# Projections of a hybrid decoder step: the two halves of the tokens in step, or one after the other

## The chip, the core and the metric

The program runs on one core of one Trainium2 chip. The metric is the device time of one execution in microseconds (us). TensorE (PE) multiplies, VectorE (DVE), ScalarE (ACT) and GpSimd (POOL) work elementwise, and SyncE (SP) starts the transfers. Every engine takes its instructions in one fixed order.

## What is computed

Two layers of a decoder trunk over 512 prompt tokens and 8 single-token samples, 1024 features wide, all in fp32. Cut to what matters here:

```python
for l in range(DEPTH):                                   # 2
    mod = silu(c) @ ada_w[l] + ada_b[l]                  # conditioning: shift, scale, gate
    h = rms_norm(x, norm_g[l]) * (1 + scale) + shift
    pa, pb, pc, pd = split(h @ w_in[l])                  # ONE input projection, 1024 -> 3648 columns
    oA = mixer_hgrn2(pa)                                 # A: chunked gated recurrence
    oB = mixer_rwkv7(pb)                                 # B: state update per token
    oC = mixer_dilated(pc)                               # C: windowed attention
    oD = mixer_pool(pd)                                  # D: pooling
    x = x + gate * (concat(oA, oB, oC, oD) @ w_out[l])   # ONE output projection, 1024 -> 1024
```

## The kernel before

Features lie on partitions and tokens along the free axis: the 512 prompt tokens and the 8 samples make 520 columns, cut into two halves of 256 and 264 (`HALF`). The input projection is cut into 29 column tiles of 128 features (`TILES`; the first, `wa`, has 64), the output projection into 8. A column tile sums over 8 feature tiles k of the input. Each fp32 operand is the sum of two parts, so one (half, k) step is three matmuls: `whi` against `hh`, `whi` against `hl`, `wlo` against `hh` (in the output projection `mh`, `ml` take the place of `hh`, `hl`). A whole column tile is 2 halves x 8 k x 3 = 48 matmuls into two PSUM tiles, one per half (`pj`; three such buffers, `pj_ps`).

Weights arrive by DMA in pieces of four k (`wraw`, six buffers). ACT copies a piece to `whi`, POOL subtracts to get `wlo` (`w_split`, L436 to L451); of either there are three buffers. So a column tile uses two pieces, k 0 to 3 and k 4 to 7, and a buffer is free again when the last matmul that reads its piece is through.

`project` (L458) issues one column tile and yields now and then the time that its matmuls take by plan, in ns. `Flow` (L124) is the planner: it lays the tensor engine's work in one order, the projections between the steps of the mixers. A mixer step of cost c allows 1.11 c ns of projection (`RATIO`, `debt`), and the projections' yields are taken from that allowance and added to the planner's clock, by which a mixer step counts as ready. Behind the planner a scheduler orders each engine's queue once more by its own estimate of when operands and buffers are there. So a change in `project` moves instructions on all engines.

When the 29 tiles are through, the projections wait for the event "mixed" (mixers A and B finished), then run the output projection over the first four k (the features of A and B), tile by tile; the last four k (C and D) come after all mixers have ended. The first layer's first seven column tiles are made in two passes of four k each (`split_projections`). Where two tiles go together (a layer's first group) `project` takes another branch.

Names of PE's instructions below: `bA` are the products of mixer B's chunks, `bR`, `bU`, `bS`, `by` the steps of its loop over 8 chunks, `bs` and `bss` sums over a head's features, `cs`, `cT`, `co` the scores, transposes and values of attention (C), `alv`, `adg`, `ao`, `sBa` parts of A and of the samples' step.

Of the kernel before, what the change touches and what calls it, by code (L numbers as in the profile page):

```python
# [18 lines left out]
PSUM = bass.MemoryType.PSUM  # L19
# [23 lines left out]
# column offsets of the parameters that sit one value per partition  # L43
# [9 lines left out]
# column tiles of the input projection, in the order in which they are made  # L53
# [70 lines left out]
class Flow:  # L124
    """Lays the tensor engine's work out in one order: projections, which are always ready, between the
    steps of the mixers, each of which waits for other engines."""
# [9 lines left out]
    def add(self, gen, prio=0):  # L136
        # priority, time when its data is there, awaited event, steps, whether it can rest here
        self.streams.append([prio, 0.0, None, gen, True])
        self.streams.sort(key=lambda e: e[0])
# [32 lines left out]
    def run(self):  # L172
        """Until the projections are through and every stream has ended."""
        while self.pj is not None or self.streams:
# [4 lines left out]
            ready = [e for e in self.streams if self._ready(e)]  # L179
# [12 lines left out]
def trunk(ctx: ExitStack, tc: tile.TileContext, I, O):  # L192
# [70 lines left out]
    def logistic(t):  # L263
        """1 / (1 + t), in place, for t = exp(-x)."""
        act(t, t, AF.Ln, bias=1.0)
        act(t, t, AF.Exp, scale=-1.0)
# [16 lines left out]
    C = {}  # L283
# [45 lines left out]
    def small_params():  # L329
        # lower bounds: cumulative softmax over the layers, minus the first layer's share  # L330
# [21 lines left out]
    modA, modS, modG = {}, {}, {}  # L352

    def ada_part(l, f0, nf, spare=0, ahead=1, pin=False):
        """Part of the conditioning, features on partitions: the shifts and scales of the feature tiles
        f0 .. f0 + nf - 1, or all the gates (nf = 8); groups of columns side by side. pin keeps the
        order of the trace, for loads that come later than the scheduler takes them to."""
# [7 lines left out]
        # a single tile: the even and the odd k side by side as well  # L365
# [35 lines left out]
        # a group is a kind of two features (nf = 4), or else one or two features of a kind  # L401
# [18 lines left out]
    def w_extend(groups, halves=(0, 1)):  # L420
        """Weight tiles [128, (k, m)] in the order of use; each comes in two halves of k."""
# [14 lines left out]
    def w_split(upto):  # L436
        """Each weight as the sum of two parts that one pass each carries."""
# [20 lines left out]
    def project(group, xt, each_k=None, k0=0, k1=8):  # L458
        """One or two column tiles, both halves of the tokens; each operand as two exact parts."""
# [3 lines left out]
        def step(i, hf, k):  # L463
# [5 lines left out]
            # a narrow tile has both parts of its weights side by side in hi  # L469
# [15 lines left out]
        else:  # L485
            step(0, 0, k0)
            yield 330.0
            for k in range(k0, k1):
                if k < k1 - 1:
                    step(0, 0, k + 1)  # L490
                step(0, 1, k)
                yield 660.0
# [10 lines left out]
    def split(hi, lo, src, eng=V):  # L503
        """Write src as the sum of two parts that one pass each carries."""
        copy(hi, src)
        sub(lo, src, hi.bitcast(F32), eng=eng)

    def evac(dst, halves):
        """Copy both halves out of PSUM, one on each of two engines."""
# [5 lines left out]
    def blk_sum(src, use, on=False):  # L515
        """Sum over the 64 features of each head, spread over them; use(psum, index). The operand goes in as
        two exact parts."""
# [21 lines left out]
    def to_tm(dst, src, other):  # L539
        """Tokens on partitions: dst[p][(., t), (c, th), d], in squares of 32; the rows are those of the head's  # L540
        parity p, or the other half."""
# [10 lines left out]
    def to_tokens(dst, src):  # L552
        """Tokens on partitions: dst[t, tile of 128 tokens, (th, p, d)]."""
# [12 lines left out]
    def scols(ap, i):  # L566
        """[.., th, b] spread over the values of batches 4 i .. 4 i + 3."""
# [3 lines left out]
    def sample_values(v, dr):  # L571
        """The samples' values [(p, v), th, b] on every partition of their parity, [(p, .), b, th, v] for four
        samples at a time, by way of DRAM."""
# [15 lines left out]
    def sample_queries(q):  # L589
        """Each sample's query per head, with zeros in the other head's rows."""  # L590
# [6 lines left out]
    def sample_read(S, z):  # L597
        """o[(p, v), th, b] = sum over keys of S[(p, key), b, th, v] q[(p, key), th, b]; both th against the
        queries of both, of which each takes its own."""
# [11 lines left out]
    # =====================================================================  # L611
# [27 lines left out]
    def again(src):  # L639
        """What waited in DRAM comes back."""  # L640
# [22 lines left out]
    def stream_A(l, L, flow):  # L663
# [4 lines left out]
        # each chunk's queries, per head with zeros in the other head's rows  # L668
# [26 lines left out]
        # the samples' step reads q, f and k as they come  # L695
# [68 lines left out]
        for cp in range(2):  # L764
            # within the chunks, and from the states before them
# [35 lines left out]
    def shift_mix(l, L, xs, dd, rows, col):  # L801
        """x + (previous token - x) * mu, into dd."""
# [28 lines left out]
    def stream_B(l, L, flow):  # L831
        yield "wa"
        a, sg = fm("ba"), fm("bsg")
        # both low ranks with their exact parts one above the other: rows hi, lo, hi against weights hi, hi, lo
# [20 lines left out]
        # decays within a chunk, relative to the chunk's middle  # L855
# [26 lines left out]
        # normalised removal key  # L882
# [14 lines left out]
        # a Newton step: the errors of the removal add up over the tokens  # L897
# [13 lines left out]
        # bonus  # L911
# [6 lines left out]
        # the samples' step  # L918
# [808 lines left out]
def pack(inp):  # L1727
# [9 lines left out]
    d = {}  # L1737
# [96 lines left out]
```

## Time and profile before

| | |
|---|---|
| Device time, median of 3 runs | 782.69 us (782.3 to 784.27) |
| Profiled execution: span from first to last instruction | 781.0 us |
| Its own device time | not listed apart from the three runs |
| Mean granted TensorE clock | 0.956 |
| PE busy | 715.5 us (92%) |
| DVE, POOL, ACT busy | 593.2 (76%), 384.7 (49%), 365.2 us (47%) |

The profile gives the busy time of each engine, its waits by what ended them, and a line of the granted clock. Times of rows are microseconds from the span's start. A matmul's row lasts 0.28 us while the next one starts 0.12 us later, since matmuls are pipelined. What PE delivers is read from the distance of starts, not from a row's duration.

### The profile page before, as it was taken

The page shows a single profiled execution, that of the slowest core. Times are in us where ns is not written, and L with a number is a line of the kernel's source. Part 1 is how long each engine was busy: PE and PEld are TensorE (multiplying, and loading weights), DVE is VectorE, ACT ScalarE, POOL GpSimd, SP SyncE. Part 2 cuts the span into 40 slices and gives each one's busy share as a digit, 9 for nine tenths or more (in the row PEclk, how much of TensorE's full clock was granted, in tenths as well). Part 3 has the DMA queues.
Part 4 walks back from the last instruction along what each step waited for, and adds up shares of the span by engine and source line. Part 5 has one row for each costly group of instructions (what it writes and reads, how often), then busy time and mean ns, then how long its engine had stood idle before and what let it go on. Part 6 is the DMA issues. An engine that isn't in the chain of part 4 may idle for free. (4 is left out here: it accounts for less than half of the span.)

```text
span 781.0 us, 18348 instructions
## 1 busy us (share of the span) xinstructions
PE 715.5 (92%) x7297; PEld 626.3 (80%) x7297; DVE 593.2 (76%) x1263; ACT 365.2 (47%) x778; POOL 384.7 (49%) x348
## 2 busy tenths in 40 slices
PE   2999989698789999999998999879889999999998
PEld 1687769487779998787888989768778989777898
DVE  4558759999998465788747897986999765587873
ACT  5233667014243465674235688412233547477520
POOL 2335427874753243236637756686554332223662
PEclk9999999897899999999998999899889999999999
DMA  9979755152232155337263323515232134135222
GB/s 330 351 276 335 226 168 153 41 163 69 82 98 56 40 183 192 125 97 272 69 190 96 118 68 98 147 56 150 69 95 86 56 99 150 56 113 163 98 77 102
DMA packets 67446, 105.74 MB, mean 135 GB/s; under 512 B 18336, under 2 KB 26848, under 8 KB 67360
## 3 DMA queue, kind: packets, MB, share of 16 engines
q1 hardware_dynamic: 67216, 104.50, 41.8%
q8 instruction: 57, 0.93, 0.5%
q14 instruction: 29, 0.24, 0.1%
q10 hardware_dynamic: 144, 0.06, 0.0%
HBM read 88.20 MB, written 14.22 MB: 131 GB/s over the span
## 5 line engine op out<-in xcount | busy, mean ns | idle before, releaser
L237 POOL TENSOR_TENSOR wlo<-wraw,whi 128x512 fp32r<-128x512 f32 x144 | 203.1, 1416 | 235.4 <-ACT whi L261 203.8
L269 PE MATMUL pj<-hh,whi 128*128 128x256 f32 (+1 forms) x928 | 278.0, 308 | 17.9 <-DVE raw L632 6.9
L269 PE MATMUL pj<-hl,whi 128*128 128x256 f32 (+1 forms) x928 | 268.3, 296 | 0.6 <-DVE hl L254 0.6
L269 PE MATMUL pj<-hh,wlo 128*128 128x264 f32 (+1 forms) x896 | 262.2, 298 | 0.5 <-POOL wlo L237 0.5
L269 PEld LDWEIGHTS pj<-hh,whi 128*128 128x128 f32 x928 | 182.3, 200 | 36.1 <-issue 12.6
L269 PEld LDWEIGHTS pj<-hl,whi 128*128 128x128 f32 x928 | 183.1, 200 | 4.6 <-issue 2.7
L269 PEld LDWEIGHTS pj<-hh,wlo 128*128 128x128 f32 x896 | 176.3, 199 | 6.2 <-issue 4.1
L261 ACT ACTIVATE whi<-wraw 128x512 fp32r<-128x512 f32 (+1 forms) x146 | 90.6, 623 | 161.5 <-PE pj L269 128.6
L269 PE MATMUL pj<-ml,whi 128*128 128x264 f32 (+1 forms) x256 | 72.5, 286 | 2.0 <-DVE cst L250 1.4
L269 PE MATMUL pj<-mh,whi 128*128 128x256 f32 (+1 forms) x256 | 72.6, 291 | 0.3 <-ACT mh L261 0.3
L269 PE MATMUL pj<-mh,wlo 128*128 128x256 f32 (+1 forms) x256 | 71.5, 283 | 0.0
L237 POOL TENSOR_TENSOR gate<-gate,raw 128x520 f32<-128x520 f32 x16 | 22.1, 1383 | 69.9 <-ACT gate L258 34.3
L254 DVE SCALAR_TENSOR_TENSOR x<-pj,mod,x 128x256 f32<-128x256 f32 x64 | 30.8, 481 | 33.1 <-PE pj L269 32.7
L269 PEld LDWEIGHTS pj<-mh,whi 128*128 128x128 f32 x256 | 47.4, 188 | 4.8 <-issue 2.6
L269 PEld LDWEIGHTS pj<-ml,whi 128*128 128x128 f32 x256 | 48.2, 188 | 3.3 <-DVE ml L237 2.7
L269 PEld LDWEIGHTS pj<-mh,wlo 128*128 128x128 f32 x256 | 48.0, 188 | 0.6 <-POOL wlo L237 0.4
L269 PE MATMUL ada<-adaw,sc 128*32 128x256 f32 (+1 forms) x448 | 33.9, 375 | 11.9 <-DVE nacc L237 11.8
L269 PEld LDWEIGHTS ada<-adaw,sc 128*32 128x32 f32 x448 | 12.4, 115 | 20.6 <-DVE nacc L237 11.8
L269 PE MATMUL alv<-aqz,ak 128*64 128x64 f32 x384 | 20.6, 249 | 6.6 <-DVE ak L237 6.6
L254 DVE SCALAR_TENSOR_TENSOR bX<-bX,bfac,bS 64x64 f32<-64x64 f32 x56 | 15.6, 279 | 14.2 <-PE bS L269 12.8
L269 PEld LDWEIGHTS alv<-aqz,ak 128*64 128x64 f32 x384 | 17.2, 157 | 10.0 <-issue 4.5
L1123 DVE COPY bUV<-bU 64x128 f32<-64x128 f32 x16 | 4.7, 295 | 23.3 <-ACT bUV L261 23.1
(409 smaller groups left out, 1456.1 us busy)
## 6 DMA issues: line engine op xcount, KB each, us to landing
wraw<-in_w_in_dram SPq DMA_DIRECT2D x112, 256.0 KB, 2.8
adaw<-in_ada_w_dram SPq DMA_DIRECT2D x48, 512.0 KB, 5.5
wraw<-in_w_out_dram SPq DMA_DIRECT2D x32, 256.0 KB, 2.8
x<-in_x_dram SPq DMA_DIRECT2D x8, 520.0 KB, 5.8
ckT<-in_ckT_dram SPq DMA_DIRECT2D x8, 320.0 KB, 3.2
x<-xmid SPq DMA_DIRECT2D x4, 520.0 KB, 5.8
cvr<-in_cvr_dram SPq DMA_DIRECT2D x4, 512.0 KB, 5.3
xmid<-x SPq DMA_DIRECT2D x7, 260.0 KB, 2.0
```

The lines of the kernel that those rows point to most:

```text
L237: return eng.tensor_tensor(out=out, in0=a, in1=b, op=op)
L254: return V.scalar_tensor_tensor(out=out, in0=a, scalar=s, in1=b, op0=op0, op1=op1)
L261: return A.activation(out, a, AF.Copy)
L269: return PE.matmul(out, lhsT, rhs, start=start, stop=stop)
L1123: V.tensor_copy(UV[ROWS[1], 1], pv[ROWS[1]])
```

## The change

In `project`, for a single column tile: before, the first half's step runs one k ahead of the second half's, so that both halves go through k together, offset by one. Now all k of the first half run, and then all k of the second half. The plan's yields change with it: before 330 and then eight times 660 (5,610 ns for a tile of 8 k; 2,970 for 4 k), now 660 after every second k (5,280 and 2,640). The rest of the diff takes out comments and does not change the program.

```diff
         else:
-            step(0, 0, k0)
-            yield 330.0
-            for k in range(k0, k1):
-                if k < k1 - 1:
-                    step(0, 0, k + 1)
-                step(0, 1, k)
-                yield 660.0
+            for hf in range(2):
+                for k in range(k0, k1):
+                    step(0, hf, k)
+                    if k % 2:
+                        yield 660.0
```

The same matmuls are issued, as many of each kind. Where they stand is seen in the order of the instructions. First PE in layer 0, between two groups of B's products (`bA`), in the kernel before; `pj_1926` and `pj_1927` are the two halves of one column tile:

```order
L269 MATMUL bA<-bZ_1694,bk 64x128
L269 MATMUL pj_1926<-hh_200,whi 128x256
L269 MATMUL pj_1926<-hl_202,whi 128x256
L269 MATMUL pj_1926<-hh_200,wlo 128x256
L269 MATMUL pj_1927<-hh_200,whi 128x264
L269 MATMUL pj_1927<-hl_202,whi 128x264
L269 MATMUL pj_1927<-hh_200,wlo 128x264
```

The same place in the kernel after; `pj_1914` is a second half:

```order
L269 MATMUL bA<-bZ_1731,bk 64x128
L269 MATMUL pj_1914<-hh_200,whi 128x264
L269 MATMUL pj_1914<-hl_202,whi 128x264
L269 MATMUL pj_1914<-hh_200,wlo 128x264
L269 MATMUL pj_1914<-hh_200,whi 128x264
L269 MATMUL pj_1914<-hl_202,whi 128x264
L269 MATMUL pj_1914<-hh_200,wlo 128x264
L269 MATMUL bA<-bZ_1728,bk 64x128
```

The alternation of the halves is gone, and mixer steps now stand inside one half. The second place is PE near the end of layer 1's attention, in the kernel before; `pj_9189`, `pj_9190` and `pj_9250` belong to the output projection:

```order
L269 MATMUL cs<-ckl,cqs 128x512
L1244 MATMUL cT<-c_ident,cS 128x128 x4
L269 MATMUL pj_9189<-ml_9184,whi 128x256
L269 MATMUL pj_9189<-mh_9183,wlo 128x256
L269 MATMUL pj_9190<-ml_9184,whi 128x264
L269 MATMUL pj_9190<-mh_9183,wlo 128x264
...
L269 MATMUL pj_9250<-mh_9183,wlo 128x256
L269 MATMUL co<-cPT,cvtm 64x128 x2
```

And in the kernel after, the end of a run that began 22 rows earlier with `cT` behind `pj_9197`:

```order
L269 MATMUL cs<-ckl,cqs 128x512
L1242 MATMUL cT<-c_ident,cS 128x128 x4
L269 MATMUL co<-cPT,cvtm 64x128 x2
L1242 MATMUL cT<-c_ident,cS 128x128 x6
L269 MATMUL co<-cPT,cvtm 64x128 x4
L1242 MATMUL cT<-c_ident,cS 128x128 x8
L269 MATMUL co<-cPT,cvtm 64x128 x6
L269 MATMUL pj_9160<-mh_9154,whi 128x256
```

There attention's steps stand with projections between them before, and without any now: 81 matmuls of the mixers in a row (34 `cT`, 30 `co`, 12 `cs`, 5 sums), and in layer 0 at the same place 75 (28 `cT`).

## Rows read from the trace of the kernel before

**Rows 1.** The page: busy time, and the granted clock in 40 slices (tenths).

```profile
PE 715.5 (92%) x7297; PEld 626.3 (80%) x7297; DVE 593.2 (76%) x1263; ACT 365.2 (47%) x778; POOL 384.7 (49%) x348
...
PEclk9999999897899999999998999899889999999999
```

**Rows 2.** Stages: stretch, length, busy PE, PEld, DVE, ACT, POOL, then clock.

```profile
113.00:243.00 130.00, 112.30 (x1345) 99.71 (x1344) 124.10 (x200) 44.38 (x85) 82.14 (x71) 0.89 0.34 100
243.00:317.00 74.00, 73.35 (x926) 63.63 (x924) 42.08 (x124) 38.24 (x93) 23.90 (x18) 1.00 0.38 120
317.00:368.00 51.00, 50.27 (x366) 41.10 (x365) 44.44 (x122) 35.55 (x89) 21.41 (x15) 0.97 0.51 171
...
480.00:608.00 128.00, 113.18 (x1308) 103.31 (x1306) 115.05 (x191) 46.31 (x87) 80.09 (x71) 0.91 0.33 98
...
684.00:736.00 52.00, 50.55 (x375) 41.49 (x371) 43.20 (x121) 36.33 (x90) 20.04 (x15) 0.97 0.42 138
```

**Rows 3.** PE's waits over the whole span: us in total, times, longest.

```profile
PE pj L269 <- DVE raw L632: 6.9, 6, 2.8
...
PE pj L269 <- ACT s L258: 3.6, 1, 3.6
...
PE pj L269 <- DVE av L512: 0.9, 1, 0.9
...
PE pj L269 <- ACT whi L261: 0.8, 2, 0.4
...
PE pj L269 <- POOL wlo L237: 0.5, 2, 0.3
```

**Rows 4.** Timeline at 380 us: start, duration, engine, instruction, idle before.

```profile
379.87 0.63 ACT L261 ACTIVATE whi<-wraw 128x512 fp32r<-128x512 f32 x1 [3.81 <-PE pj L269]
...
380.09 0.28 PE L269 MATMUL pj<-mh,whi 128*128 128x256 f32 x1
...
380.56 0.28 PE L269 MATMUL pj<-ml,whi 128*128 128x256 f32 x1
...
380.58 1.28 POOL L237 TENSOR_TENSOR wlo<-wraw,whi 128x512 fp32r<-128x512 f32 x1 [2.70 <-ACT whi L261]
```

**Rows 5.** DVE's waits from 480 to 608 us.

```profile
DVE bMB L237 <- PE bA L269: 5.8, 3, 4.9
```

**Rows 6.** DVE by line, 317 to 368 us: busy, mean ns, idle before.

```profile
L1228 DVE CUSTOM_DVE_ANT_0 cS<-cs,c_atab 128x256 f32<-128x256 f32 (+3 forms) x14 | 7.1, 514 | 2.0 <-PE cs L269 1.9
L250 DVE TENSOR_SCALAR cS<-cS,cst 128x256 f32<-128x256 f32 (+3 forms) x14 | 5.8, 436 | 0.1
L237 DVE TENSOR_TENSOR bslo<-bsq,bshi 128x520 fp32r<-128x520 f32 x2 | 3.4, 1700 | 1.2 <-ACT bshi L261 1.2
L237 DVE TENSOR_TENSOR by<-by,again 128x520 f32<-128x520 f32 x4 | 3.3, 844 | 0.0
...
L250 DVE TENSOR_SCALAR cst<-cst 128x1 f32<-128x1 f32 x14 | 1.9, 145 | 0.0
L1233 DVE RECIPROCAL cst<-cst 128x1 f32<-128x1 f32 x14 | 1.9, 153 | 0.9 <-ACT cS L258 0.9
...
L237 DVE TENSOR_TENSOR by<-by,bsq 128x1040 f32<-128x1040 f32 x1 | 1.2, 1233 | 0.0
L237 DVE TENSOR_TENSOR ml<-by,mh 128x1040 fp32r<-128x1040 f32 x1 | 1.2, 1226 | 0.0
...
L251 DVE TENSOR_SCALAR by<-by,par 128x520 f32<-128x520 f32 x2 | 1.0, 542 | 0.0
```

**Rows 7.** PE's attention steps by timeline, 343 to 367 us.

```profile
343.31 1.09 PE L1244 MATMUL cT<-c_ident,cS 128*128 128x128 f32 x8
...
351.65 0.50 PE L269 MATMUL cs<-ckl,cqs 64*128 64x512 f32 x1
352.08 0.51 PE L269 MATMUL cs<-cks,cqs 128*128 128x512 f32 x1
...
366.75 1.09 PE L269 MATMUL co<-cPT,cvtm 128*64 128x128 f32 x14
```

## The prediction, made before the changed kernel ran

> **What bounds the kernel now.** The page comes first. PE is busy for 715.5 of 781.0 us and DVE for 593.2 [rows 1], so PE looks like the only bound, but that is an average. Read by stages, the two layers show the same four stretches [rows 2]. From 113 to 243 us, and again from 480 to 608, DVE is busy for 124.1 of 130 and 115.1 of 128 us, while PE leaves 130 - 112.3 = 17.7 and 128 - 113.2 = 14.8 us idle and its clock is at 0.89 and 0.91 in the mean. There DVE sets the pace: mixer B's preparation and A's chunks. Next comes the loop over B's chunks, from 243 to 317 us in layer 0: PE 73.4 of 74 at full clock, DVE only 42.1. Then B's end and attention, 317 to 368 and 684 to 736: PE busy for 50.3 of 51 and 50.6 of 52 us, but DVE for 44.4 and 43.2 as well. There both are nearly bounds, PE by a little. What is left, mostly the output projection, is PE's.
>
> The reader is to see that a projection matmul has three prices. In a stretch that PE sets it costs its distance of starts: four steps from 380.09 to 380.56, 0.1175 us each [rows 4]. Where DVE sets the pace and PE waits, it is free. And where it is the filler between the steps of a mixer, taking it away saves time only until DVE is the bound.
>
> **The change part by part.** The matmuls and their weight loads are the same in number, 48 for a column tile and 24 for a pass of four k. What moves is their place, and there are four effects.
>
> *PSUM.* Before, the first half of a tile is complete 6 matmuls before the tile's end, and the next tile needs that buffer 6 matmuls after its start: 12 x 0.1175 = 1.4 us for ACT and DVE to empty it. After it is 48 matmuls, 5.6 us. PE's waits for readers of PSUM are 6.9 (raw), 3.6 (s) and 0.9 (av), 11.4 us in all [rows 3], the longest 3.6, and 3.6 + 1.4 is still below 5.6. I expect nearly all of them to go. Their worth is between 0 and 11.4 us. I take 0, since the raw and av waits lie where DVE sets the pace and the one for s stands behind ACT's own queue just ahead of it; whatever PE gains there it waits for at the next mixer step.
>
> *Weights.* Before, the piece of k 0 to 3 is released at the middle of a tile, and the piece that takes its buffer is needed in the middle of the next: 48 matmuls, 5.6 us. After it is released at three quarters and needed at one quarter of the next tile: 24 matmuls, 2.8 us. Behind the release stand `whi` on ACT and `wlo` on POOL, 379.87 to 381.86, 2.0 us when both engines are free [rows 4]. So 0.8 us of slack is left where tiles follow each other directly, and in the order mixer steps stand between most tiles. PE's waits for `whi` and `wlo` are 1.3 us now [rows 3]. The cost lies between 0 and 24 us: with one more POOL subtraction of 1.28 us in front, a tile is late by 0.5 us, and there are 48 tiles of 8 k. I take 0, because POOL is busy half the time [rows 1].
>
> *The plan.* A tile of 8 k counts 5,280 instead of 5,610, so the same allowance buys 6% more projection matmuls between mixer steps. Counted in the order, 44 more stand ahead of the first step of B's chunk loop (`bR`) in layer 0 and 51 more in layer 1. Those fall into the two stretches that DVE sets, and PE has 17.7 and 14.8 us idle there: worth 44 x 0.1175 = 5.2 and 51 x 0.1175 = 6.0 us at most, nothing at least, if each of them delays what DVE waits for. In layer 1 some do: DVE waits 5.8 us for `bA` [rows 5], and 9 to 15 more matmuls stand ahead of each group of it; 13 x 0.1175 = 1.5 us. In layer 0 DVE hardly waits (5.9 of 130 us). I take -5.2 - 6.0 + 1.5 = -9.7 us.
>
> *Where they are missing.* In the chunk loop there are 21 and 45 more, behind the attention 28 and 29 more, so between the end of that loop (`bS`) and the last `co` there are 93 fewer in layer 0 (91 instead of 184) and 125 fewer in layer 1 (60 instead of 185). If PE stayed the bound, these stretches would shrink by 10.9 and 14.7 us, and the gain of 9.7 would stand. But the plan's tiles run out earlier, and the output projection waits for B. The order shows a run of mixer steps without any projection in each layer. PE's time for it, in layer 0: 28 `cT` at 1.09 / 8 = 0.136 (3.8 us), 30 `co` at 1.09 / 14 = 0.078 (2.3), 12 `cs` and 5 sums at 352.08 - 351.65 = 0.43 (7.3), in all 13.4 [rows 7]; in layer 1, with 34 `cT`, 14.2. DVE in the same run: 6 halves of scores at 514 + 436 + 145 + 153 ns = 1.25 (7.5 us), and B's end, 3.4 + 1.2 + 1.0 + 3.3 + 1.2 = 10.1, in all 17.6 [rows 6]. The excess is 4.2 and 3.4 us, and at the end of each run one half's chain of 1.25 us has nothing beside it. Sum: 4.2 + 3.4 + 2.5 = 10.1 us lost. It is 0 if DVE has run ahead, and at most all that was freed, 25.6. I take 10.1, nearer to what DVE needs than to either end.
>
> *Clock.* In the attention stretches the clock is at 0.97 now [rows 2]: 0.03 x 51 = 1.5 us lost in a low spell. PE's new gaps there should bring one such spell more in each layer: 3.0 us. It is between 0 and 9, three spells each.
>
> The sum against the profiled execution: 781.0 - 9.7 + 10.1 + 3.0 = 784.4 us of span. The median of the runs is 1.7 above that span, so 786.1 us. The own range of this case is 781 to 791.
>
> **The rivals.**
> *Faster, by the plan.* The -9.7 come and attention stays covered, since its steps of DVE could run while PE still has the chunk loop: 782.7 - 9.7 = 773.0, and with a part of the loss 776. For it: DVE is busy for only 42.1 of 74 us in the chunk loop just ahead [rows 2]. Against it: in the order attention's scores now start at the end of the chunk loop, where in layer 0 one of the eight steps stood well before it.
>
> *No change.* The scheduler had already drawn the halves apart in many tiles of the kernel before, so the change does little more than its planned times do, and the two terms of the plan cancel: -9.7 + 10.1, 783.1. For it: they are of one size. Against it: the gaps and the clock come on top.
>
> *Much slower, by the weights.* The 2.8 us decide: where POOL or ACT holds another instruction of over 0.8 us at the release, PE waits at a tile's first quarter. At 0.3 us for each of 48 tiles that is 14 us, 797. For it: POOL waits for ACT and ACT for PE, both in a fixed order. Against it: only 1.3 us of waits now.
>
> *Faster, by PSUM and the clock.* The waits for readers of PSUM go and time goes with them: 782.7 - 11.4 = 771.3. They and the other waits of the two DVE stretches hold the clock at 0.89 and 0.91, 14.3 and 11.5 us lost; the 7.8 us for raw and av are a quarter of the 32.5 us idle, so 6 us of clock more, 765. For it: the waits are real. Against it: DVE is 95% busy around them. The Trainium skill, in TensorE: Matmul & The Clock Gate, section "A second HAM failure mode: psum-queue depth-cycling", says that small gaps of PE between groups of matmuls that cycle through PSUM banks let the clock fall and rise again and again, and that this costs throughput. By that rule the change should raise the clock in both stretches, and the sum would lose its sign; the trace agrees that the clock is low there, but not that PE's pace counts there.
>
> **How the numbers follow.** The likeliest case has 0.55, with 786.1 us; faster by the plan 0.25, no change 0.10, the weights 0.06, PSUM and clock 0.04. About 0.3% of 782.69 us, 2.35 us, is what a measurement can tell from no change: from 780.3 to 785.0. Of the likeliest case 0.34 lies above that, 0.20 within, 0.01 below. Slower: 0.34 + 0.06 = 0.40, and 0.02 for no change turned worse, 0.42. Within: 0.20 + 0.08 = 0.28. Faster: 0.25 + 0.04 + 0.01 = 0.30. Range: 775, where the gain stands almost whole, to 797, where the weights decide or half of the freed 25.6 us is lost; about a tenth on either side is left out.
>
> **What would show it.** Right: the waits for raw, s and av almost gone; PE's idle time from 113 to 243 down by about 5 us with DVE as busy as now; in each layer a stretch of some 17 us at attention's end in which PE waits for DVE (`cT` for `cS`, sums for `bslo`) and the clock falls. Wrong: if those stretches have PE near 100% busy, the attention term fails and the kernel is faster; if PE waits for `whi` or `wlo` by more than 3 us, the weights' term fails; if DVE's busy share from 480 to 608 falls below 0.88, the extra projections stood in its way and the gain fails.

## The result, and the profile after

The kernel after takes 806.45 us (median of 4 runs, 805.12 to 807.46) and the kernel before, run beside it, 783.48 us: a ratio of 1.0259, 95% interval 1.0222 to 1.0295. It is slower, as forecast, but by 23 us and not by 3, and outside the range. The profiled execution has a span of 803.3 us against 781.0, so 22.3 us are to be found.

The page of the kernel after, busy time and granted clock, beside [rows 1]:

```profile
PE 721.4 (90%) x7297; PEld 629.9 (78%) x7297; DVE 585.9 (73%) x1263; ACT 366.1 (46%) x778; POOL 381.7 (48%) x348
...
PEclk9799999899989898997999999999999999989799
```

PE has the same 7,297 matmuls. Its busy time rises by 5.9 us and its idle time from 781.0 - 715.5 = 65.5 to 803.3 - 721.4 = 81.9 us: 16.4 of the 22.3 us are idle time of PE, though the change was to put more filler where PE idles.

To see where, the span is cut at the same events in both kernels. Only the first cut, 113.00 us, is a time: the first `bs`, at 112.90 us before, comes at 114.75 after. The end of the first stretch is the first `bU` of mixer B's loop, since it needs the whole preparation; the first `bR`, by which the prediction counted, doesn't, and the scheduler has put 63 small matmuls of the preparation (`bXT`) behind it in layer 0. The columns are those of [rows 2]; the last two, the share of the DMA engines and GB/s, are not used here. The kernel before: preparation, loop over chunks, attention, output projection of layer 0, then the first three of layer 1:

```profile
113.00:244.78 131.78, 114.08 (x1359) 101.35 (x1357) 125.83 (x202) 45.02 (x86) 82.59 (x72) 0.90 0.34 98
244.78:316.89 72.11, 71.46 (x909) 61.88 (x910) 40.27 (x121) 37.50 (x91) 23.45 (x18) 1.00 0.39 123
316.89:367.84 50.95, 50.22 (x365) 41.05 (x365) 44.51 (x122) 35.54 (x88) 21.41 (x15) 0.97 0.51 170
367.84:415.62 47.78, 47.78 (x393) 42.25 (x393) 30.22 (x68) 15.30 (x24) 24.29 (x19) 1.00 0.46 144
...
478.69:613.15 134.46, 119.64 (x1415) 109.36 (x1414) 121.08 (x200) 49.63 (x94) 83.75 (x74) 0.91 0.33 98
613.15:682.24 69.09, 67.14 (x842) 58.32 (x845) 40.32 (x115) 35.59 (x84) 20.96 (x17) 1.00 0.32 94
682.24:736.41 54.17, 52.72 (x402) 42.26 (x402) 44.84 (x128) 37.17 (x92) 20.04 (x15) 0.97 0.41 134
```

The same stretches of the kernel after:

```profile
113.00:253.14 140.14, 120.16 (x1433) 108.83 (x1427) 123.77 (x203) 50.16 (x96) 85.56 (x74) 0.91 0.33 97
253.14:335.39 82.25, 80.54 (x919) 69.08 (x918) 42.16 (x117) 39.30 (x94) 26.36 (x21) 0.92 0.37 114
335.39:381.50 46.11, 40.16 (x271) 30.11 (x271) 38.91 (x122) 29.90 (x78) 13.17 (x11) 0.89 0.51 169
381.50:431.35 49.85, 49.85 (x421) 45.79 (x422) 33.74 (x72) 15.61 (x25) 24.05 (x20) 1.00 0.45 133
...
495.16:638.02 142.86, 124.08 (x1505) 114.42 (x1503) 128.17 (x213) 53.89 (x102) 87.87 (x77) 0.94 0.32 96
638.02:714.84 76.82, 75.98 (x894) 64.26 (x893) 43.67 (x130) 43.06 (x104) 25.74 (x19) 1.00 0.39 123
714.84:756.13 41.29, 35.86 (x227) 26.26 (x227) 32.99 (x98) 25.33 (x64) 9.31 (x8) 0.79 0.25 80
```

The reader is to see lengths and idle time together. In layer 0's preparation PE is busy 6.1 us longer, and its idle time has not fallen but risen, from 17.7 to 20.0 us. Both attention stretches are shorter, with PE idle for 6.0 and 5.4 us where it was 0.7 and 1.5. Counting the projection matmuls in each stretch from the trace gives a price for each that came or went:

| Stretch | length, us | projections | us per projection |
|---|---|---|---|
| Preparation, layer 0 / 1 | +8.4 / +8.4 | +64 / +55 | 0.13 / 0.15 |
| Loop over chunks, layer 0 / 1 | +10.1 / +7.7 | +12 / +39 | see below / 0.20 |
| Attention, layer 0 / 1 | -4.8 / -12.9 | -93 / -125 | 0.05 / 0.10 |
| Output projection, layer 0 / 1 | +2.1 / +2.6 | +28 / +29 | 0.07 / 0.09 |
| Layer 1's beginning | +0.7 | +2 | |

The lengths add up to 22.3 us. The distance of starts is 0.1175 us [rows 4]. So a projection that was put ahead cost about its distance or more (in layer 0's preparation, counted from the first `bs`, 52 more came with 6.5 us, 0.125 each), and one that was missing in the attention gave back less.

In layer 1 other work moved too, so its prices are not of projections alone. The preparation got 32 matmuls `alv` that stood in the loop before, and DVE is busy there for 128.2 us instead of 121.1, with 13 instructions more. 47 matmuls, mostly of the samples' attention (`csv`, `csn`) and of scores, went from the attention into the loop, and DVE's busy time in the attention fell from 44.8 to 33.0 us. Loop and attention of layer 1 are best read together: 5.2 us shorter, with 86 projections fewer.

### The profile page after: what moved, and what is told of

The parts are those of the page before. It is cut to its first block, busy times and chain, and to the rows that moved or that the text cites. A ratio compares the mean times of both kernels' runs of the same rounds, so it can differ in the third digit from the quotient of the medians.

```text
span 803.3 us, 18313 instructions
## 1 busy us (share of the span) xinstructions
PE 721.4 (90%) x7297; PEld 629.9 (78%) x7297; DVE 585.9 (73%) x1263; ACT 366.1 (46%) x778; POOL 381.7 (48%) x348
## 4 chain that ended last, share of the span: by engine, by line
PE 59%; DVE 29%; issue 4%; ACT 3%; DMA 2%; POOL 1%; SPq 0%; DVEq 0%; ACTq 0%; POOLq 0%
PE pj L269 38%; PE ada L269 3%; DVE bZ L237 3%; PE by L269 2%; PE cs L269 2%; DVE bTp L237 2%; PE bs L269 1%; PE co L269 1%; PE cT L1242 1%; DVE bslo L237 1%; DVE aqz L237 1%; DVE bX L546 1%; PE bS L269 1%; DVE raw L630 1%; DVE bsq L987 1%
## 5 line engine op out<-in xcount | busy, mean ns | idle before, releaser
L237 POOL TENSOR_TENSOR wlo<-wraw,whi 128x512 fp32r<-128x512 f32 x144 | 200.8, 1400 | 262.4 <-ACT whi L261 231.6
L269 PE MATMUL pj<-hh,whi 128*128 128x256 f32 (+1 forms) x928 | 272.5, 303 | 16.8 <-DVE raw L630 4.9
L269 PE MATMUL pj<-hl,whi 128*128 128x256 f32 (+1 forms) x928 | 265.2, 293 | 0.7 <-POOL hl L237 0.7
L269 PEld LDWEIGHTS pj<-hh,whi 128*128 128x128 f32 x928 | 179.3, 197 | 34.8 <-issue 11.1
L269 PEld LDWEIGHTS pj<-hl,whi 128*128 128x128 f32 x928 | 180.5, 197 | 4.2 <-issue 1.8
L269 PEld LDWEIGHTS pj<-hh,wlo 128*128 128x128 f32 x896 | 174.1, 196 | 5.5 <-issue 2.5
L269 PE MATMUL pj<-ml,whi 128*128 128x256 f32 (+1 forms) x256 | 72.3, 284 | 0.0
L269 PE MATMUL pj<-mh,wlo 128*128 128x256 f32 (+1 forms) x256 | 72.1, 283 | 0.0
L269 PEld LDWEIGHTS alv<-aqz,ak 128*64 128x64 f32 x384 | 17.9, 166 | 18.7 <-issue 10.1
L269 PEld LDWEIGHTS ada<-adaw,sc 128*32 128x32 f32 x448 | 14.8, 124 | 21.2 <-DVE nacc L237 12.0
L1242 PE MATMUL cT<-c_ident,cS 128*128 128x128 f32 x80 | 16.0, 334 | 10.6 <-DVE cst L250 5.9
```

The lines of the kernel that those rows point to most:

```text
L237: return eng.tensor_tensor(out=out, in0=a, in1=b, op=op)
L269: return PE.matmul(out, lhsT, rhs, start=start, stop=stop)
L1242: PE.transpose(pT[:, 128 * j:128 * j + 128], S[n][:, pp, 128 * j:128 * j + 128], ident)
```

## The experiments

Two theories stood at the start. *Plan*: the loss comes from the planned times, which put more projections ahead. *Halves*: it comes from the new order of the matmuls in a tile (PSUM, weights). Later the question was whether the loss is a price for each projection put ahead, or whether any order other than that of the kernel before loses.

**The change in two parts.** The halves one after the other, with the planned times of before (against the kernel after):

```diff
-            for hf in range(2):
-                for k in range(k0, k1):
-                    step(0, hf, k)
-                    if k % 2:
-                        yield 660.0
+            order = [(hf, k) for hf in range(2) for k in range(k0, k1)]
+            step(0, *order[0])
+            yield 330.0
+            for i in range(1, len(order), 2):
+                for hf, k in order[i:i + 2]:
+                    step(0, hf, k)
+                yield 660.0
```

> The halves one after the other as in the change, but the planned times as before: 330 after the first (half, k) step, then 660 after every two, 5,610 for a tile of 8 k. The number of projection matmuls ahead of each mixer step is then again that of the kernel before (959 instead of 1003 ahead of the first bR). Theory 'plan' (the shorter planned times put more projections ahead of the mixers, and these are paid in full in the stretches I took to be set by DVE): 783 us, within 4 of the kernel before. Theory 'halves' (the order inside a tile costs: weight pieces held longer, mixer steps standing elsewhere): 800 to 808 us, as the changed kernel.

And the halves in step as before, with the planned times of after, 660 behind every second step (the added lines alone, against the kernel before):

```diff
+            order = [(0, k0)]
+            for k in range(k0, k1):
+                if k < k1 - 1:
+                    order.append((0, k + 1))
+                order.append((1, k))
+            for i in range(0, len(order), 2):
+                for hf, k in order[i:i + 2]:
+                    step(0, hf, k)
+                yield 660.0
```

> The two halves in step as before, but the planned times of the change: 660 after every two (half, k) steps, 5,280 for a tile. The first bR has 1005 projection matmuls ahead of it, as in the changed kernel (1003). Theory 'plan': 803 to 810 us, all of the change's loss. Theory 'halves': 780 to 787 us.

The first takes 785.76 us, ratio 1.0008 (0.9984 to 1.0033); the second 802.96, 1.0228 (1.0211 to 1.0244). The order of the halves, by itself, costs and gives nothing that can be measured, and the planned times alone carry most of the loss, 2.28 of 2.59%.

**Less filler with the new times, and more weight buffers.** The kernel after with `RATIO = 1.045`, and the kernel after with its weight buffers at `"wraw": 4, "wpart": 4` instead of 6 and 3:

> The changed kernel with the allowance RATIO 1.045 in place of 1.11, so that a mixer step buys as many projection matmuls as before (1.11 x 5280 / 5610 = 1.045); the planner's clock still runs 6% short. 987 projection matmuls stand ahead of the first bR in layer 0 and 2782 in layer 1 (before 959 and 2740, changed 1003 and 2791). Theory 'plan' by the number of projections ahead: a third to a half of the loss comes back, 794 to 800 us. Theory 'halves': 803 to 808 us.

> The changed kernel with four buffers each for whi and wlo instead of three, and four instead of six for the raw pieces (SBUF has no room for more). A piece's buffer then has 48 matmuls more before it is needed again. If the shorter slack of the weight pieces is what costs: under 795 us. Theory 'plan': no better than 802 us, since PE waits only 3.3 us for whi and wlo in the changed kernel.

The ratio 1.045 gives 792.77 us, 1.0105 (1.0077 to 1.0134): 13.7 of the 23 us come back. Four buffers give 808.45, 1.0311 (1.0283 to 1.0338). PE's waits for `whi` and `wlo` fall there from 3.3 to 0.6 us and the time does not, so they are not what is lost; that this kernel also has two `wraw` buffers fewer was not separated.

The trace with four buffers shows one thing more. Its layer 0's preparation, from 113.00 to 246.01 us, has 51 projections more than that of the kernel before and is 1.2 us longer, with DVE busy for 124.7 us, where the kernel after has 64 more and is 8.4 us longer; DVE does not wait for `bA` in it. So the number of projections put ahead does not set the price. Layer 1 lost what layer 0 gained: its preparation takes 146.7 us, against 142.9 in the kernel after.

**Only the allowance.** The planner's clock runs as before, the allowance as after:

```diff
-        self.t += c
+        self.t += c * 5610 / 5280
```

> The changed kernel, where the planner's clock advances by the old times (x 5610 / 5280) and only the allowance is charged the short ones. 987 projection matmuls ahead of the first bR in layer 0, 2791 in layer 1 (before 959 and 2740, changed 1003 and 2791), B's loop ends at 1304 and 3130 (before 1256 and 3016, changed 1321 and 3112). Theory 'projections ahead of the mixers are paid': 795 to 805 us. Theory 'the planner's clock, which takes results to be late': 783 to 790 us.

It takes 801.6 us, 1.017 (1.0096 to 1.0244). So the larger allowance carries about two thirds of the loss (0.4 to 0.9 of it by the interval). The moment at which a mixer step counts as ready carries part of it too: with the allowance of before and only the planner's clock short, which is the kernel with 1.045 above, 1.05% are left.

**What sets the pace of a stretch?** Two kernels leave out the product `wlo` x `hh` of some column tiles of the kernel before, those made in the preparation (352 matmuls fewer) or those of the loop (224 fewer); `THIN` lists the tiles:

```diff
-            ops = [(hi, xhi), (hi, xlo)] + ([(lo, xhi)] if M == 128 else [])
+            ops = [(hi, xhi), (hi, xlo)] + ([(lo, xhi)] if M == 128 and key[1] not in THIN else [])
```

> The kernel before, where the 11 column tiles aq0 to cq0 of each layer (those that PE works on from 113 to 241 and 480 to 608 us) leave out their third product, wlo against hh, so that these columns lack the low part of their weights. 22 x 16 = 352 matmuls less, 41.4 us of PE at 0.1175 each; planned times as before. Theory 'DVE sets the pace' (the step of the prediction): PE only waits longer there, 780 to 785 us. Theory 'one chain' (PE's fixed order puts the projections ahead of what DVE waits for, so each is paid there too): 15 to 41 us less, under 770 us, with DVE's busy share in these stretches up.

> The same cut for the 7 tiles cq1 to cg1 of each layer, which stand in the loop over B's chunks and at its end, where PE is busy 99%: their columns lack the low part of their weights. 14 x 16 = 224 matmuls less, 26.3 us. Both theories: PE sets the pace here, 757 to 763 us. It is the price of a projection matmul where nobody doubts it, beside the run on the stretch before.

Both miss on the slow side: 794.67 us, 1.0112 (1.0083 to 1.014), and 790.49, 1.0049 (1.0015 to 1.0083). With less work on PE the kernel is slower. The two preparations of the first of them:

```profile
113.00:243.76 130.76, 94.54 (x1202) 84.54 (x1201) 125.71 (x205) 44.40 (x87) 80.64 (x72) 0.82 0.34 99
479.95:625.55 145.60, 103.15 (x1278) 93.45 (x1276) 135.83 (x208) 51.42 (x99) 87.91 (x74) 0.84 0.31 92
```

In layer 0, PE is busy 19.5 us less and the stretch is 1.0 us shorter, with DVE busy as before (125.7 and 125.8 us). So DVE did set the pace there, as the prediction read it. That is a statement on less work for PE, and it does not carry over to more. In layer 1 the stretch is 11.1 us longer, and DVE's own busy time is up by 14.8 us.

**Filler the other way.** The halves order with the old times and `RATIO = 1.0`:

> The halves one after the other with the old planned times, and RATIO 1.0 in place of 1.11: a mixer step buys 10% fewer projection matmuls than before. 930 stand ahead of the first bR (before 959). If the price of projections ahead of the mixers goes on in this direction: 772 to 779 us, faster than both. If the kernel before stands where the two prices balance (PE waits more ahead of bR, less cover behind): 783 to 792 us.

It takes 807.58 us, 1.0278 (1.023 to 1.0327), outside both expectations. Fewer projections ahead lose as much as more.

**One layer.** Halves order in both, new times in layer 0, old ones in layer 1 (`old`; the removed lines are left out):

```diff
+            order = [(hf, k) for hf in range(2) for k in range(k0, k1)]
+            old = group[0][0][0] == 1
+            if old:
+                step(0, *order.pop(0))
+                yield 330.0
+            while order:
+                for hf, k in order[0:2]:
                     step(0, hf, k)
+                order = order[2:]
+                yield 660.0
```

> Halves order in both layers, but the planned times: layer 0 as in the kernel after (660 every two k steps), layer 1 as in the kernel before (330, then 660 each). The order of layer 0's matmuls is then that of the kernel after (first bR behind 1,003 projection matmuls, 959 before), that of layer 1 that of before (2,735 against 2,740). If the loss sits in the stretches and each pays for its own order, layer 0 keeps its part (+5.8 +12.8 -4.8 +2.1 = +15.9 us over the first layer's stretches after normalisation) and layer 1 comes back: 799 to 804 us, and layer 1's stretches within 2 us of those before. If the two layers hang together (a state carried over from layer 0), layer 1's stretches differ from before by 5 us or more and the sum is anywhere between 786 and 808.

It takes 805.59 us, 1.026 (1.0204 to 1.0316). Layer 0's preparation and loop in its trace:

```profile
113.00:254.38 141.38, 116.97 (x1432) 105.76 (x1426) 127.79 (x204) 50.47 (x96) 86.29 (x75) 0.95 0.33 96
254.38:336.79 82.41, 80.57 (x919) 68.95 (x918) 41.45 (x116) 39.36 (x93) 26.05 (x21) 0.92 0.36 114
```

Layer 0 repeats its loss (17.3 us up to its end, 15.9 expected). Layer 1, in the order of before, is still 9.3 us longer than in the profiled execution of before, and 2.8 us longer than in that of the halves with the old times, which has the same order there. But this profiled execution took 809.37 us, where the median is 805.59, and that of the halves with the old times 789.46, where it is 785.76. By the medians the run is 21.9 us above the kernel before; less the 17.3 of layer 0, some 5 us are left for layer 1. So the new times in layer 0 alone cost nearly as much as in both, and the layers add up only roughly. Why layer 1 gains so little by its old order was not settled.

**Blocks of filler by hand.** A helper runs n steps of the projections (6 matmuls each) without counting them in the plan. It stands, in turn, ahead of mixer B's substitution on DVE, ahead of each `bA` product, and in the loop ahead of each `bU`, in the kernel before. The three places of the call are shown together, and cut:

```diff
+        def ahead(n):
+            t, debt = flow.t, flow.debt
+            for _ in range(n):
+                flow._step_pj()
+            flow.t, flow.debt = t, debt
...
+        ahead(8)
         for t in range(1, 16):
...
         for tl in range(4):
+            ahead(2)
             products(bt, tl, 0)
...
+            ahead(1)
             p = mm_ps("bU")
```

> The kernel before, with 48 projection matmuls of each layer brought forward in one block to the place right before the 15 substitution steps on VectorE (mixer B), without counting them in the plan; nothing else is reordered by hand, and at the end as many are missing in the attention. First bR then stands behind 1,019 (before 959) in layer 0. Theory 1 (my prediction's step: matmuls put ahead there are free, VectorE sets the pace): the two VectorE-set stretches keep 128.6 and 129.5 us, the attention loses what the kernel after lost (-4.8, -12.9): 768 to 783 us. Theory 2 (TensorE and VectorE form one chain there; each matmul ahead costs its 0.1175 us): +5 to +6 us in each of those stretches, about as much saved later: 783 to 790 us. Theory 3 (any order other than the one before loses in more places than the block's): 792 us or more, with the loops of chunks longer by 5 us or more.

> The kernel before, with 12 projection matmuls brought forward ahead of each of the four bA products that VectorE waits for (48 in each layer), not counted in the plan. Theory 1 (VectorE's waits for bA, 0.2 us before in layer 0 and 5.3 in the kernel after, are what the plan's extra filler costs): VectorE's wait for bA grows by 4 to 6 us in each layer, the stretch by the same, and e12 is 8 to 12 us slower than e11. Theory 2 (one chain, place does not matter): as e11 within 3 us. Theory 3 (any other order loses elsewhere): 792 us or more.

> The kernel before, with 6 projection matmuls brought forward in each of the eight chunks, between bR and bU of mixer B, in each layer (48 per layer), not counted in the plan. Theory 1 (price by the pitch): each chunk's chain is longer by 6 x 0.1175 = 0.7 us, a loop by 5.6 us (75.3 to 81, 74.0 to 80), about as much or more saved in the attention: 780 to 788 us. Theory 2 (the loop loses more than the pitch, as in the kernel after, where 20 more projections, 84 more matmuls in all, went with 12.8 us and a clock of 0.92 against 1.00): the loop of layer 0 88 us or more, the sum 790 to 800 us.

They take 808.57 us, 1.0286 (1.0227 to 1.0345); 814.18, 1.0358 (1.0305 to 1.0412); and 797.82, 1.0148 (1.0093 to 1.0202). Preparation, loop and attention of layer 0 with the block ahead of the substitution:

```profile
113.00:249.65 136.65, 118.79 (x1462) 106.81 (x1460) 128.48 (x211) 48.61 (x93) 86.57 (x76) 0.94 0.33 98
249.65:323.95 74.30, 72.13 (x849) 61.41 (x850) 38.90 (x113) 36.73 (x90) 23.13 (x16) 0.93 0.38 121
323.95:375.26 51.31, 44.90 (x290) 34.78 (x292) 41.73 (x117) 32.27 (x81) 16.43 (x13) 0.83 0.46 157
```

54 more projections in the preparation: +4.9 us, 0.09 each, with PE idle for 17.9 us as before (17.7). The filler did not go into the idle time. With them 49 mixer matmuls came ahead out of the loop (`alv`, `srd`), and the loop, with 10 projections fewer as well, is 2.2 us longer; over both stretches 44 more cost 7.1 us, 0.16 each. By its time the run is the third theory's, though the loop of layer 0 did not grow by the 5 us that it named. 77 fewer in the attention: +0.4 us; PE's idle time there went from 0.7 to 6.4 us and its clock from 0.97 to 0.83. With the block among the products, the same preparation:

```profile
113.00:256.03 143.03, 120.31 (x1409) 108.19 (x1409) 125.33 (x203) 47.65 (x91) 84.08 (x74) 0.89 0.33 95
```

49 more there: +11.3 us, 0.23 each, and DVE's wait for these products (us in total, times, longest) is 5.2 us, where layer 0 of the kernel before had 0.2:

```profile
DVE bMB L237 <- PE bA L269: 5.2, 2, 2.6
```

So the place counts, as theory 1 had it in layer 0, though by less than it said (5.6 us between the two kernels, not 8 to 12). In layer 1 the wait fell instead, from 5.8 to 1.8 us, and the stretch still grew by 9.7. The block in the loop: 48 more in layer 0 for +7.1 us, 0.15 each, and its attention, with 37 projections fewer and 34 other matmuls more, is 2.3 us longer. The loop's 7.1 us are near the first theory's 5.6, and the time of the whole run is the second's. Over the whole run each of the three costs more than the 11.3 us that its 96 matmuls make by the pitch: 25, 30 and 14 us, in the order above.

**A price, or a narrow optimum?** The kernel before with other ratios and nothing else changed (1.10, 1.13, 1.045 and 1.18 for 1.11):

> The kernel before with the filler's ratio at 1.10 instead of 1.11. First bR stands behind 952 projection matmuls of layer 0 (959 before) and the last bS behind 1,208 (1,256); layer 1 within 5 either way. If the cost is a smooth price of the filler ahead (about 0.12 us for each projection matmul more, less given back in the attention), so small a step moves the time by at most 5 us: 779 to 787 us. If the order of before is a lucky one and any other is worse, 790 to 805.

> The kernel before with the ratio at 1.13. First bR behind 960 (959 before) and 2,739 (2,740), last bS behind 1,227 (1,256) and 3,040 (3,016): nearly the counts of before with the steps in other places. Smooth price: within 3 us of before, 780 to 787. Lucky order: 790 to 805.

> The kernel before with the ratio at 1.045, the ratio by which the kernel after fills as much as before at 1.11. First bR behind 969 and 2,731, last bS behind 1,208 and 3,010. Smooth price: 778 to 786 (fewer in the loop of layer 0 by 58, at 0.12 us, given back in the attention). Lucky order: 790 to 808.

> The kernel before with the ratio at 1.18: about as much filler as the kernel after has (6% more for each allowance), by another way. First bR behind 967 (959) and 2,770 (2,740), last bS behind 1,256 (1,256) and 3,055 (3,016), so about a third of the shift of the kernel after. Smooth price: a third of its 23 us, 786 to 794 us. Lucky order: as slow as the kernel after, 800 to 812.

| Ratio, old planned times | us | against before |
|---|---|---|
| 1.00 (halves order) | 807.58 | 1.0278 (1.023 to 1.0327) |
| 1.045 | 807.34 | 1.0266 (1.0207 to 1.0325) |
| 1.10 | 787.45 | 1.0033 (1.0001 to 1.0065) |
| 1.11 | the kernel before | 1 |
| 1.13 | 789.39 | 1.0057 (1.0026 to 1.0087) |
| 1.18 | 805.3 | 1.0234 (1.0177 to 1.029) |

The last row has the allowance of the change by another way: 1.11 x 5,610 / 5,280 = 1.179, and 805.3 us against 806.45. It loses as much, though only 8 projections more stand ahead of layer 0's first `bR` where the change has 44 more. A price for each projection put ahead is refuted by this and by the rows with less filler, which lose as much; "any other order loses 5 us or more" is refuted by 1.10 and by the halves with the old times. The ratio 1.13 lies between its two expectations. What the table shows is a narrow valley: a ratio off by 0.01 or 0.02 costs 0.3 and 0.6%, one off by 0.065 or more over 2%, in either direction. No ratio was run in between, so it is not shown whether the loss grows steadily or in a jump. None of the versions beats the kernel before.

The ratio 1.045, layer 0, shows how less filler loses. Preparation, loop, attention, output projection:

```profile
113.00:246.48 133.48, 113.37 (x1386) 101.36 (x1384) 122.45 (x204) 45.40 (x87) 83.65 (x72) 0.94 0.33 97
246.48:314.77 68.29, 63.47 (x797) 54.77 (x797) 36.53 (x99) 34.12 (x80) 18.03 (x14) 0.98 0.31 90
314.77:372.63 57.86, 55.07 (x415) 44.37 (x415) 45.11 (x138) 38.23 (x96) 19.99 (x16) 0.97 0.45 147
372.63:425.02 52.39, 52.39 (x428) 46.53 (x428) 31.61 (x73) 15.73 (x25) 27.27 (x22) 1.00 0.56 187
```

The loop, which PE filled to 71.5 of 72.1 us before, now has 58 projections fewer (6.8 us by the pitch), and 54 of the other matmuls fewer, and is only 3.8 us shorter, with 4.8 us of idle time; attention and output projection, where they went, are 6.9 and 4.6 us longer.

## Why the prediction was wrong

**The step that failed** is in *The plan*: "Those fall into the two stretches that DVE sets, and PE has 17.7 and 14.8 us idle there". The projections were costed as free there, 1.5 us for both layers; the two preparations became 16.8 us longer. That is 15 of the 19 us by which the span was missed; the loop is 10 more, and shorter attention and output projection take 7 back. DVE set the pace, and PE was idle, and neither means that a matmul more is free. PE takes its instructions in one order, so its idle time stands at the head of certain steps, and filler put elsewhere can come in front of a step that DVE waits for. DVE is then late with what PE waits for next. PE's waits in layer 0's preparation before, and DVE's for `bA`:

```profile
PE sBa L269 <- DVE sBt L237: 7.0, 2, 4.7
PE alv L269 <- DVE ak L237: 3.9, 3, 3.2
PE pj L269 <- DVE raw L632: 3.5, 4, 2.4
...
DVE bMB L237 <- PE bA L269: 0.2, 1, 0.2
```

PE's and DVE's waits in the same stretch after:

```profile
PE alv L269 <- DVE ak L237: 5.8, 4, 2.2
PE tok L557 <- DVE av L510: 4.5, 1, 4.5
PE pj L269 <- DVE raw L630: 3.0, 2, 2.0
PE svT L575 <- DVE svc L573: 2.2, 1, 2.2
...
PE sBa L269 <- DVE sBt L237: 2.0, 2, 1.6
...
DVE bMB L237 <- PE bA L269: 5.3, 3, 2.2
DVE aqz L237 <- PE alv L269: 3.1, 1, 3.1
```

The filler did shorten one wait (`sBa`, 7.0 to 2.0 us). But DVE now waits 5.3 us for `bA` and 3.1 for `alv`, together about what the stretch grew by, and PE waits for `av`, `svc` and longer for `ak`. The block among the products makes the same wait of DVE by hand (5.2 us), and with four weight buffers, where the wait is missing, the stretch hardly grew; so that part is shown. It is not the only part: with the allowance alone, and with the block ahead of the substitution, the stretch grew by 4.3 and 4.9 us without more of that wait. That the other new waits follow from it was only read from the rows.

In layer 1 the step failed in another way. DVE's wait for `bA`, 5.8 us before, is gone, and 7.1 of the 8.4 us by which the stretch grew are more busy time of DVE itself. It also waits for the samples' values, which come back from DRAM by a transfer:

```profile
DVE sAk L237 <- DMA sv<-sv1A: 6.3, 2, 5.0
```

Which part of the 7.1 us is the 13 more instructions and which is longer ones was not taken apart. The sign that the prediction named for this failure, a busy share of DVE below 0.88 from 480 to 608 us, does not tell it: layer 1 begins 16.5 us later now, and between the same events the share is 0.90 in both kernels. In layer 0 it fell from 0.95 to 0.88.

**The loop** was costed by the pitch, 2.5 + 5.3 us, and became 10.1 + 7.7 us longer. Of the 10.1 in layer 0, 12 projections make 1.4; the clock fell from 1.00 to 0.92 (0.08 x 82 = 6.6 us). PE was idle there for only 1.7 us, and a fall without much idle time the prediction did not consider. In layer 1 39 projections make 4.6 of 7.7, at full clock; 13 other matmuls more stand there too, and the rest was not settled.

**Where they are missing** held in layer 0: the attention was to be 4.0 us shorter and was 4.8. In layer 1 it was to be 8.6 shorter and was 12.9, but work that moved into the loop is part of that, so the term was not tested cleanly there. Behind the attention 4.7 us came where 6.7 were forecast. The unfilled run is there as described. PE, 364 to 376 us in the kernel after:

```profile
364.36 0.50 PE L269 MATMUL cs<-ckl,cqs 64*128 64x512 f32 x1
364.78 0.66 PE L1242 MATMUL cT<-c_ident,cS 128*128 128x128 f32 x4
365.37 0.44 PE L269 MATMUL co<-cPT,cvtm 128*64 128x128 f32 x4
368.39 0.87 PE L1242 MATMUL cT<-c_ident,cS 128*128 128x128 f32 x3 [2.58 <-DVE cst L1231]
372.44 0.87 PE L1242 MATMUL cT<-c_ident,cS 128*128 128x128 f32 x3 [3.17 <-DVE cst L250]
```

Here PE waits for DVE's softmax of the next half (`cst`), 2.6 and 3.2 us, as the sum had it; the clock in the two attention stretches is 0.89 and 0.79.

**PSUM.** "I expect nearly all of them to go" was wrong, and taking their worth as 0 was right. PE's waits over the whole span, beside [rows 3]:

```profile
PE pj L269 <- DVE raw L630: 4.9, 5, 2.0
...
PE pj L269 <- ACT s L258: 3.5, 1, 3.5
...
PE pj L269 <- ACT whi L261: 2.4, 2, 1.4
...
PE pj L269 <- POOL wlo L237: 0.9, 1, 0.9
```

8.4 of 11.4 us are still there. The rule of the Trainium skill on PSUM cycling (TensorE: Matmul & The Clock Gate, "A second HAM failure mode: psum-queue depth-cycling") was the ground of one rival; the clock in the preparations rose from 0.90 and 0.91 to 0.91 and 0.94, and both became longer. Since most of the waits stayed, the case hardly tests the rule; it gives it no weight.

**Weights.** Their waits rose from 1.3 to 3.3 us, just over the bound of 3 that the prediction named. But a fourth buffer gave nothing and the halves with the old times cost nothing, so the term of 0 stands.

**Of the rivals** none named a large loss by the plan. The sum had part of that loss inside it, as a bound: nothing gained, "if each of them delays what DVE waits for", which would be 5.2 + 6.0 = 11.2 us for the two preparations; they grew by 16.8, beyond the bound. It took the other end because DVE hardly waited in layer 0 (5.9 of 130 us). That inference was wrong: that DVE hardly waits says how the plan of before times its operands, and not that they could come later.

## What to carry to other kernels

Idle time of an engine with one fixed order is not by itself room for filler. In none of the runs that put more projections into a preparation did PE's idle time there fall by more than 0.6 us. Right ahead of the instruction that waits it might be room; that was not tried. Before an added step is costed at nothing, look at which step of the other engine it comes in front of, and price it at its full pitch if that one is on the chain. And a number that paces a static plan (here the planned time of a step) is a tuned value: a change that shifts it by 6% should be compared with the plan's own ratio moved by 6%, before anything else is read into it.

## What the runs showed of the hardware

PE's clock fell in a stretch in which the profile has PE busy throughout. In the loop of the kernel after (columns as above):

```profile
253.60:260.40 6.80, 6.80 (x83) 6.20 (x81) 6.65 (x13) 1.06 (x3) 4.08 (x4) 1.00 0.21 49
260.40:267.20 6.80, 6.80 (x45) 5.72 (x45) 1.74 (x9) 3.09 (x8) 0.00 (x0) 0.56 0.08 31
```

A mean of 0.56 is nearly all at 1.2 GHz, and 45 matmuls begin there where 83 did just before, without idle time of PE in either; shortly ahead of the fall stood 16 matmuls of 4 columns (`srd`, from 258.75 for 1.95 us). That they are its cause was not tested. The prediction had the clock fall by idle time alone.

An elementwise instruction with two operands on DVE takes up to nearly twice as long when one of POOL is already running, and its usual time when it starts first; then POOL's takes longer. Timeline of the kernel before (start, duration, engine, instruction): the same instruction of POOL (`aq`) in both layers, ahead of one of DVE in layer 0 and behind one of the same size in layer 1. DVE's takes 1.23 us alone ([rows 6], `by<-by,bsq`).

```profile
131.55 1.30 POOL L237 TENSOR_TENSOR aq<-aq,raw 128x520 f32<-128x520 f32 x1
131.63 2.31 DVE L237 TENSOR_TENSOR bkk<-bkk,brn 128x1040 f32<-128x1040 f32 x1
```

```profile
496.89 1.23 DVE L237 TENSOR_TENSOR brn<-brn,bsq 128x1040 f32<-128x1040 f32 x1
497.11 2.16 POOL L237 TENSOR_TENSOR aq<-aq,raw 128x520 f32<-128x520 f32 x1 [1.38 <-DVE raw L632]
```

Of DVE's 31 instructions of this size in the kernel before, 11 start while a `TENSOR_TENSOR` of POOL has more than 0.3 us to go: ten take 1.48 to 2.37 us, one 1.24. The other 20 take 1.22 to 1.25 us. The Trainium skill (SBUF — State Buffer, section "SBUF: two separate sides") says that the two engines share a pair of ports, which an instruction of POOL that reads SBUF, or one of DVE with both operands in SBUF, holds alone for its whole length, whichever starts first; the trace agrees, with 2.31 against 1.23 us. It makes DVE's part of a stretch depend on when POOL works: with the same instructions in the preparation of layer 1, and a few more, DVE was busy for 121.1 us in the kernel before and 135.8 in the one with 352 matmuls fewer. How much of that is POOL was not taken apart.
